# A decoder trunk on one core: the mixer's value products 512 columns wide over four open banks, and another order of its products

## The chip, the cores and the metric

One Trainium2 chip, of which the kernel uses one core. The metric is the device time of one execution in microseconds. The kernel before took 1346.19 us (median of 3 runs, 1345.29 to 1346.24). Engines are named as in the profile: PE is TensorE's matrix multiply, PEld its weight load, DVE is VectorE, ACT ScalarE, POOL GpSimd, SP SyncE, which here only starts transfers.

## The reference, cut to what matters

The trunk runs 512 tokens of width 1024 through two mixer layers, each followed by a dense SwiGLU layer, all in float32. The change touches only the first mixer, which has two groups of heads side by side:

```
h = rms_norm(x, w);  z, xbc, dt, q, k, v, g, gk = split(h @ w_in)
# group 1 (SSD): 16 heads of 64, here 8 pairs of 128 rows
xs, B, C = silu(conv(xbc));  dt, a from dt_raw
y = (causal C.B with decay) @ (xs*dt) + C @ states + d_skip*xs
y = rms_norm over 512 columns (y * silu(z))     # pairs 0-3, pairs 4-7
# group 2 (GLA): 4 heads, keys of 128, values of 256
o = (causal q.k with decay) @ v + q @ states
o = rms_norm over 256 columns (o) * silu(g)
x = x + concat(y, o) @ w_out
```

## The kernel before

Activations lie with features on the partitions and tokens along the free side, so a tile is 128 x 512. Every dense product is done in three passes over operands split in two (`mm3`, L167: high by high, high by low, low by high), and every 512 KB of weights goes through `weight` (L146): a transfer on SP's queue into `wraw` (two buffers), ACT's cast to `whi`, DVE's subtraction to `wlo` (three buffers each). A dense product of 128 output rows (`dense`, L172) is 24 products of 128 x 512 into one PSUM bank. There are eight banks: three that rotate for dense products (`acc`, L63) and, in the mixer, five for helpers (`aux`, L76: st, a1, xt once, a2 twice).

Group 1 runs in eight pairs f = 0..7. For each pair:

- `conv` (L409): the x product and the convolution on DVE, which gives `xs`; `z_gate` (L452): the z product and its SiLU, which gives `zg`.
- `core_in` (L458): decay factors `mt`, `ea`, `cd` on ACT, four transposes of `xs` on PE, and from these `xdt` and `xde` on DVE.
- `core_states` (L496): PE's state products (L501), then ACT's copy of the first state (L505) and four short DVE steps (L508), which give `hs`.
- `core_out` (L515): PE's outputs (L521, which waits until `hs` is complete, and L529), then four DVE steps to `y`.
- `finish` (L567): the squares of `y`, and after pairs 3 and 7 `group_norm` (L539): `rstd` (L197) sums over the partitions with two PE products (L205, L206), takes the inverse root in ten DVE steps (L210 to L220), then four scalings (L543), and each scaled tile is split by ACT (`mxh`, L140) and DVE (`mxl`, L141).

The scaled tiles feed the output projection: `out_round(r, ...)` (L309) is one quarter of it, 96 products in eight banks of 12, whose results DVE adds to the residual x (L319). Rounds 0 and 1 need pairs 0 to 3 and pairs 4 to 7, rounds 2 and 3 the GLA heads.

`values(h)` (L549) makes the 256 value columns of GLA head h with tokens on the partitions: for each of four token blocks one bank, 24 products that move 256 weight columns against a block of x, and ACT's scaled copy into `v` (L561). Four heads are 384 products.

The order on each engine is made at build time by a scheduler that takes, among what it holds for ready, what the program wrote first (weights are taken earlier than written, `AHEAD`). `order(i, behind)` adds that i stands behind another instruction on PE. Engines then run their own queue in order and wait at semaphores. In the program x and z products are written one pair ahead: in step f come `conv(f + 1)`, `core_states` of f, `z_gate(f + 1)`, `core_out` of f. `values(0)` is written in step 1, `values(1)` behind pair 3, round 0 in step 7, `values(2)` and `values(3)` behind pair 7. Group 2 follows: `project(0)` (L656: the q and k products of a head, 48 products), round 1, `project(1)`, then `inner` (L707) and `outer` head by head. Four products of the gate (L644, on bank st, from `gw`) are written at the start of group 2.

Of the kernel before, what the change touches and what calls it, by code (L numbers as in the profile page):

```python
# [8 lines left out]
F32 = mybir.dt.float32  # L9
# [9 lines left out]
P = 128  # L19
# [27 lines left out]
def kernel(ctx: ExitStack, tc: tile.TileContext, A, yT, stop=99):  # L47
# [28 lines left out]
    def aux(tag="st"):  # L76
        while isinstance(phase["tags"][tag], str):
            tag = phase["tags"][tag]
        return phase["p"].tile([P, T], F32, tag=tag, name=nm(tag), bufs=phase["tags"][tag])
# [66 lines left out]
    def weight(src, kc, m):  # L146

        with tc.high_priority(offset=AHEAD):
            return weight_now(src, kc, m)
# [17 lines left out]
    def mm3(out, ah, al, bh, bl, first, last):  # L167
        E.matmul(out, ah, bh, start=first, stop=False)  # L168
        E.matmul(out, ah, bl, start=False, stop=False)  # L169
        return E.matmul(out, al, bh, start=False, stop=last)  # L170
# [106 lines left out]
    def tok_scalar(R):  # L277

        ps = aux()
        for c in range(4):  # L280
            E.transpose(ps[:, c * P:(c + 1) * P], R[:, c * P:(c + 1) * P], ident)
        r = const.tile([P, 4], F32, tag="rtok", name=nm("rtok"))
        V.tensor_copy(r, ps.rearrange("p (c x) -> p c x", c=4)[:, :, 0])
        return r

    def gate(pool, tag, ps, R, bufs):

        h = pool.tile([P, T], F32, tag="cva", name=nm(tag + "h"), bufs=2)
# [20 lines left out]
    def out_round(r, parts, nxt=None):  # L309

        mms = []
        for m2 in range(4):
            w = weight(A["w_out"][r, m2], 4, 256)
            for j in range(2):
                m = 2 * m2 + j
                ps = acc()
                mms += dense(ps, (w[0][:, :, j * P:(j + 1) * P], w[1][:, :, j * P:(j + 1) * P]), parts)
                with tc.high_priority(offset=FREE):
                    V.tensor_tensor(X[m], X[m], ps, ALU.add)  # L319
                if nxt is not None:  # L320
                    nxt.add(m)
        return mms
# [8 lines left out]
    with tc.tile_pool(name="gkp", bufs=1) as gkp:  # L331
# [70 lines left out]
        with tc.tile_pool(name="ssd", bufs=2) as sp:  # L402
# [26 lines left out]
            def group(g):  # L429

                bank = (lambda: aux("a2")) if g == 0 else acc
                return conv(8 + g, "bT", 1, bank), conv(10 + g, "cT", 2, bank)
# [19 lines left out]
            def z_gate(f):  # L452
                w = weight(A["w_z"][f], KD, P)
                ps = acc()
                zmm[f] = dense(ps, w, xp)
                return gate(sp, "z", ps, R, 2)

            def core_in(f, xs, cb, behind=None):  # L458

# [36 lines left out]
            def core_states(part, btok, behind):  # L496

                f, xs, mt, ea, cd, xdt, xde = part
                pst = aux("a2")
                for c in range(3):  # L500
                    i = E.matmul(pst[:, c * P:(c + 1) * P], btok[:, c, :],  # L501
                                 xde[:, c].rearrange("p h e -> p (h e)"), start=True, stop=True)
                    order(i, behind, "states behind products that run until x is ready")
                hs = sp.tile([P, 3, P], F32, tag="hs", name=nm("hs"), bufs=1)
                S.copy(hs[:, 0, :], pst[:, 0:P])  # L505
                for c in (1, 2):
                    for h in range(2):
                        ready = V.scalar_tensor_tensor(hs[:, c, 64 * h:64 * h + 64],  # L508
                                               hs[:, c - 1, 64 * h:64 * h + 64],
                                               cd[:, c - 1, h:h + 1],  # L510
                                               pst[:, c * P + 64 * h:c * P + 64 * h + 64],
                                               ALU.mult, ALU.add)
                return hs, ready

            def core_out(part, state, zg, cT, behind):  # L515

                hs, ready = state
                f, xs, mt, ea, cd, xdt, xde = part
                po = aux("a2")
                for c in range(3):  # L520
                    i = E.matmul(po[:, c * P:(c + 1) * P], hs[:, c, :], cT[:, (c + 1) * P:(c + 2) * P],  # L521
                                 start=True, stop=True)
                    order(i, behind, "outputs behind products that run until the states are ready")
                    wait_for(i, ready, "outputs in one go")
                end = i
                pd = aux("a2")
                for c in range(4):
                    for h in range(2):
                        i = E.matmul(pd[64 * h:64 * h + 64, c * P:(c + 1) * P], xdt[:, c, h, :],  # L529
                                     mt[:, h, c, :], start=True, stop=True)  # L530
                        order(i, end, "outputs in one go")
                y = sp.tile([P, T], F32, tag="y", name=nm("y"), bufs=5)
                V.scalar_tensor_tensor(y, xs, col("d_skip", f), pd, ALU.mult, ALU.add)
                V.tensor_tensor(ea, po[:, :3 * P], ea, ALU.mult)
                V.tensor_tensor(y[:, P:], y[:, P:], ea, ALU.add)
                V.tensor_tensor(y, y, zg, ALU.mult)
                return y, i
# [10 lines left out]

            def values(h):  # L549

                mms = []
                wv = [weight(A["w_v"][h, j], 4, 256) for j in range(2)]
                v = gkp.tile([P, 4, 256], F32, name=f"v{h}")
                for i in range(4):
                    ps = acc()
                    for k in range(KD):
                        wh, wl = wv[k // 4]
                        xh, xl = xp[k]
                        mms.append(mm3(ps[:, :256], xh[:, i * P:(i + 1) * P], xl[:, i * P:(i + 1) * P],
                                       wh[:, k % 4, :], wl[:, k % 4, :], k == 0, k == KD - 1))  # L560
                    S.activation(v[:, i, :], ps[:, :256], AF.Copy, scale=rtok[:, i:i + 1])  # L561
                vt[h] = v
                return mms

            rounds, ys, sums_sq = [], [], []

            def finish(f, y):  # L567

                ys.append(y)
                sq = res.tile([P, T], F32, tag="sq", name=nm("ysq"), bufs=2)  # L570
                S.activation(sq, y, AF.Square)
                if f % 4:
                    V.tensor_tensor(sq, sums_sq[-1], sq, ALU.add)
                sums_sq.append(sq)
                if f % 4 == 3:
                    rounds.append(group_norm(f // 4, ys[-4:], sq))
# [15 lines left out]
            y, end = core_out(part, hs, zg[0], cT, zmm[2][7])  # L592
            part = core_in(1, xs[1], cb, end)
            finish(0, y)
            rtok = tok_scalar(R)
            v = values(0)
            hs = core_states(part, btok, v[5])
            y, end = core_out(part, hs, zg[1], cT, v[27])
            part = core_in(2, xs[2], cb, end)
            finish(1, y)  # L600
            for f in range(2, 8):
                cT_out = cT
                if f < 7:
                    if f == 3:
                        bc = group(1)
                    xs[f + 1] = conv(f + 1, "xs", 3)
                    hs = core_states(part, btok, mm[f + 1][4])
                    if f == 3:
                        cb, cT, btok = spread(*bc, mm[f + 1][-1])
                    zg[f + 1] = z_gate(f + 1)  # L610
                    last = zmm[f + 1][-1]
                else:
                    mms = out_round(0, rounds[0])
                    hs = core_states(part, btok, mms[3])
                    last = mms[11]
                y, end = core_out(part, hs, zg[f], cT_out, last)
                if f < 7:
                    part = core_in(f + 1, xs[f + 1], cb, end)
                finish(f, y)
                if f in (3, 7):  # L620
                    values(1 if f == 3 else 2)
            values(3)


        with tc.tile_pool(name="gla", bufs=2) as gp:
# [721 lines left out]
```

## Time and profile before

| | |
|---|---|
| median of 3 runs | 1346.19 us |
| the profiled execution | 1345.15 us, span 1343.0 us |
| PE busy | 1333.1 us (99%), 6506 products |
| PEld busy | 1094.3 us (81%) |
| DVE busy | 812.6 us (61%) |
| ACT busy | 564.5 us (42%) |
| moved by DMA | 122.23 MB, 91 GB/s |
| granted TensorE clock | 1.0 throughout |

The mixer's group 1 lies from the start of the span to about 223 us, group 2 from there to about 404 us. A row of the timeline has the start, the duration, the engine, the source line, the operation, the tile written and the tiles read (for PE the moving operand first, then the stationary one), sizes, and a count where several follow each other. The brackets hold the idle time of that engine ahead of it and what ended it. Durations of PE's products overlap, since the next one starts while the last one drains: what a product costs in a stream is the distance of the starts. One of the program's small float32 products appears as two passes in the profile (three L501 products as x6).

### The profile page before, as it was taken

Reading aid. Unit: us, or ns where it says so; the run is one execution under the profiler, and the core shown is the slowest. Engines: PE = TensorE matmul, PEld = TensorE weight load, DVE = VectorE, ACT = ScalarE, POOL = GpSimd, SP = SyncE. Lnnn points to the kernel's source line nnn. Section 1 sums busy time; section 2 is a strip of 40 time slices with the busy share of each in tenths; the row PEclk is TensorE's granted clock in tenths of the full one; section 3 lists DMA queues with packets and bytes.
Section 4 is the critical chain, followed back from the end, with each engine's and each line's share of the span. In section 5 each row is a group of like instructions: output and inputs, shape, how many; then the busy total and the mean of one; then the engine's idle time right before and its main releaser. Section 6 shows DMA issues by size and latency. Waiting matters only on the chain.

```text
span 1343.0 us, 16690 instructions
## 1 busy us (share of the span) xinstructions
PE 1333.1 (99%) x6506; PEld 1094.3 (81%) x6506; DVE 812.6 (61%) x1387; ACT 564.5 (42%) x958; POOL 7.8 (1%) x35
## 2 busy tenths in 40 slices
PE   9999999999999999999999999999999999999998
PEld 6888889888888888888888887777788888888887
DVE  7888977778976444444333469987674444443221
ACT  7675625544343232322222338886543322222111
POOL 0000000000000000000000000000000000000000
PEclk9999999999999999999999999999999999999999
DMA  5343232222223333333333321110223333333331
GB/s 180 127 126 95 81 100 86 96 66 63 80 96 98 104 94 94 94 94 98 95 101 103 91 79 47 53 48 32 63 92 97 94 94 95 104 100 94 114 108 61
DMA packets 36782, 122.23 MB, mean 91 GB/s; under 512 B 4768, under 2 KB 5792, under 8 KB 36704
## 3 DMA queue, kind: packets, MB, share of 16 engines
q1 hardware_dynamic: 35888, 120.72, 29.0%
q8 instruction: 51, 0.84, 0.3%
q10 hardware_dynamic: 816, 0.46, 0.1%
q14 instruction: 27, 0.22, 0.1%
HBM read 119.03 MB, written 2.13 MB: 90 GB/s over the span
## 4 chain that ended last, share of the span: by engine, by line
PE 87%; DVE 6%; ACT 5%; issue 1%; DMA 1%; POOL 0%; SPq 0%; DVEq 0%; POOLq 0%; ACTq 0%
PE acc L168 27%; PE acc L170 26%; PE acc L169 26%; PE sco L1095 1%; ACT whi L160 1%; ACT sc L1108 1%; DVE wlo L161 1%; PE po L1142 1%; PE ptr L1123 1%; DVE sc L1106 1%; PE a L529 1%; ACT mt L472 1%; PE a L753 1%; DVE cva L421 0%; PE a L521 0%
## 5 line engine op out<-in xcount | busy, mean ns | idle before, releaser
L160 ACT CAST whi<-wraw 128x1024 fp32r<-128x1024 f32 (+2 forms) x221 | 225.7, 1022 | 560.0 <-PE acc L169 430.4
L168 PE MATMUL acc<-xh,whi 128*128 128x512 f32 x1144 | 450.4, 394 | 0.2 <-ACT qT L1070 0.2
L169 PE MATMUL acc<-xl,whi 128*128 128x512 f32 x1144 | 446.6, 390 | 0.0
L170 PE MATMUL acc<-xh,wlo 128*128 128x512 f32 x1144 | 446.4, 390 | 0.0
L161 DVE TENSOR_TENSOR wlo<-wraw,whi 128x1024 fp32r<-128x1024 f32 (+2 forms) x221 | 262.0, 1187 | 150.4 <-ACT whi L160 150.0
L168 PEld LDWEIGHTS acc<-xh,whi 128*128 128x128 f32 x1144 | 215.0, 188 | 44.7 <-issue 0.8
L170 PEld LDWEIGHTS acc<-xh,wlo 128*128 128x128 f32 x1144 | 215.0, 188 | 44.8
L169 PEld LDWEIGHTS acc<-xl,whi 128*128 128x128 f32 x1144 | 215.1, 188 | 44.0 <-issue 0.4
L823 DVE TENSOR_TENSOR fu<-acc,R 128x512 f32<-128x512 f32 x44 | 30.4, 691 | 137.7 <-PE acc L170 137.7
L169 PE MATMUL acc<-fhl,whi 128*128 128x512 f32 x288 | 112.2, 390 | 0.0
L168 PE MATMUL acc<-fhh,whi 128*128 128x512 f32 x288 | 112.2, 390 | 0.0
L170 PE MATMUL acc<-fhh,wlo 128*128 128x512 f32 x288 | 112.2, 390 | 0.0
L820 DVE TENSOR_TENSOR fg<-acc,R 128x512 f32<-128x512 f32 x44 | 30.4, 691 | 89.3 <-PE acc L170 89.3
L169 PEld LDWEIGHTS acc<-fhl,whi 128*128 128x128 f32 x288 | 54.1, 188 | 11.3
L168 PEld LDWEIGHTS acc<-fhh,whi 128*128 128x128 f32 x288 | 54.1, 188 | 11.2
L170 PEld LDWEIGHTS acc<-fhh,wlo 128*128 128x128 f32 x288 | 54.1, 188 | 11.0
L168 PE MATMUL acc<-mxh,whi 128*128 128x512 f32 x128 | 49.9, 392 | 0.0
L169 PE MATMUL acc<-mxl,whi 128*128 128x512 f32 x128 | 49.8, 390 | 0.0
L170 PE MATMUL acc<-mxh,wlo 128*128 128x512 f32 x128 | 49.7, 390 | 0.0
L1108 ACT ACTIVATE sc<-sc,mx 128x128 f32<-128x128 f32 (+3 forms) x64 | 35.5, 558 | 11.7 <-DVE mx L1106 11.6
L1095 PE MATMUL sco<-kT,qT 96*128 96x256 f32 (+3 forms) x128 | 39.6, 440 | 0.7 <-ACT qT L1070 0.7
L837 DVE TENSOR_TENSOR x<-x,acc 128x512 f32<-128x512 f32 x16 | 11.0, 688 | 42.9 <-PE acc L170 42.9
(355 smaller groups left out, 1601.9 us busy)
## 6 DMA issues: line engine op xcount, KB each, us to landing
wraw<-in_w_gate_dram SPq DMA_DIRECT2D x44, 512.0 KB, 3.5
wraw<-in_w_up_dram SPq DMA_DIRECT2D x44, 512.0 KB, 3.5
wraw<-in_w_down_dram SPq DMA_DIRECT2D x32, 512.0 KB, 3.6
wraw<-in_w_out_dram SPq DMA_DIRECT2D x16, 512.0 KB, 3.5
wraw<-in_w_xbc_dram SPq DMA_DIRECT2D x12, 512.0 KB, 3.8
wraw<-in_w_down_dram SPq DMA_DIRECT2D x16, 384.0 KB, 3.1
wraw<-in_w_z_dram SPq DMA_DIRECT2D x8, 512.0 KB, 3.5
wraw<-in_w_v_dram SPq DMA_DIRECT2D x8, 512.0 KB, 3.5
```

The source lines that it names most:

```text
L160: S.copy(hi[:, :kc * m], r)
L161: i = V.tensor_tensor(lo[:, :kc * m], r, hi.bitcast(F32)[:, :kc * m], ALU.subtract)
L168: E.matmul(out, ah, bh, start=first, stop=False)
L169: E.matmul(out, ah, bl, start=False, stop=False)
L170: return E.matmul(out, al, bh, start=False, stop=last)
L472: S.activation(mt[:, h, c, :], acb[:, h, c * P:(c + 1) * P], AF.Relu, scale=-1.0, bias=act[:, c, 2 * f + h:2 * f + h + 1])
L529: i = E.matmul(pd[64 * h:64 * h + 64, c * P:(c + 1) * P], xdt[:, c, h, :], mt[:, h, c, :], start=True, stop=True)
L753: i = E.matmul(po[e][:, r * P:(r + 1) * P], v[:, r, e * P:(e + 1) * P], sc[:, r, :], start=True, stop=(r == 0))
L820: V.tensor_tensor(g, pg, R, ALU.mult)
L823: V.tensor_tensor(u, pu, R, ALU.mult)
L1095: i = E.matmul(ps[:, at:at + n], self.qts[j][:, b * P:(b + 1) * P], self.kts[j][:, :n], start=True, stop=True)
L1108: S.activation(sc[:, at:at + n], sc[:, at:at + n], AF.Exp, bias=mx[:, j:j + 1], scale=-1.0, accum_out=sm[:, j:j + 1])
```

## The change

Three things change, all in group 1.

1. `values(h)` now makes heads h and h + 1 together. Weights of both heads are laid side by side, so that a product moves 512 columns (256 of each head). A weight tile holds two of the eight k chunks for both heads; all four token blocks are open at once, in the three `acc` banks and a1, and the weight tiles are gone through one after the other. Each tile comes in two transfers of 256 KB in place of one of 512 KB. The four banks are complete only in the last quarter; then ACT copies each bank in two halves (eight copies in a row). There are 192 products of 512 columns in place of 384 of 256.
2. x and z products are written two pairs ahead: step f has `conv(f + 2)`, `core_states` of f behind its fifth product, `z_gate(f + 2)`, `core_out` of f. `zg` gets a third buffer.
3. Step 6 has no x and z products left and takes round 0; step 7 takes `values(2)` (heads 2 and 3). `values(0)` (heads 0 and 1) and the transposes for its token factors come behind pair 3. Nothing is written behind pair 7 any more: `project(0)` and round 1 follow at once.

```diff
-                return gate(sp, "z", ps, R, 2)
+                return gate(sp, "z", ps, R, 3)
...
-                wv = [weight(A["w_v"][h, j], 4, 256) for j in range(2)]
-                v = gkp.tile([P, 4, 256], F32, name=f"v{h}")
+                vt[h], vt[h + 1] = (gkp.tile([P, 4, 256], F32, name=f"v{h + e}") for e in range(2))
+                banks = [acc() for _ in range(3)] + [aux("a1")]
+                for q in range(4):
+                    raw = wp.tile([P, KD * P], F32, tag="wraw", name=nm("wraw"), bufs=2)
+                    with tc.high_priority(offset=AHEAD):
+                        for e in range(2):
+                            nc.sync.dma_start(raw.rearrange("p (k e m) -> p k e m", k=2, e=2)[:, :, e, :],
+                                              A["w_v"][h + e, q // 2, :, 2 * (q % 2):2 * (q % 2) + 2])
+                        wh, wl = parts(raw, 2, T)
+                    for i in range(4):
+                        for k in range(2):
+                            xh, xl = xp[2 * q + k]
+                            mms.append(mm3(banks[i], xh[:, i * P:(i + 1) * P], xl[:, i * P:(i + 1) * P],
+                                           wh[:, k, :], wl[:, k, :], (q, k) == (0, 0), (q, k) == (3, 1)))
                 for i in range(4):
-                    ps = acc()
-                    for k in range(KD):
...
-                    S.activation(v[:, i, :], ps[:, :256], AF.Copy, scale=rtok[:, i:i + 1])
-                vt[h] = v
+                    for e in range(2):
+                        S.activation(vt[h + e][:, i, :], banks[i][:, 256 * e:256 * e + 256], AF.Copy,
+                                     scale=rtok[:, i:i + 1])
...
-            rtok = tok_scalar(R)
-            v = values(0)
-            hs = core_states(part, btok, v[5])
-            y, end = core_out(part, hs, zg[1], cT, v[27])
-            part = core_in(2, xs[2], cb, end)
-            finish(1, y)
-            for f in range(2, 8):
+
+            for f in range(1, 8):
                 cT_out = cT
...
+                if f < 6:
+                    xs[f + 2] = conv(f + 2, "xs", 3)
+                    fill = mm[f + 2]
+                elif f == 6:
+                    fill = out_round(0, rounds[0])
                 else:
-                    mms = out_round(0, rounds[0])
-                    hs = core_states(part, btok, mms[3])
-                    last = mms[11]
+                    fill = values(2)
+                hs = core_states(part, btok, fill[4])
...
+                if f < 6:
+                    zg[f + 2] = z_gate(f + 2)
+                    last = zmm[f + 2][-1]
+                else:
+                    last = fill[11]
                 y, end = core_out(part, hs, zg[f], cT_out, last)
                 if f < 7:
                     part = core_in(f + 1, xs[f + 1], cb, end)
                 finish(f, y)
-                if f in (3, 7):
-                    values(1 if f == 3 else 2)
-            values(3)
+                if f == 3:
+                    rtok = tok_scalar(R)
+                    values(0)
```

Three places on PE show what the order became. The first is the value products. Before, behind pair 0's outputs, `whi` and `wlo` are the moved weights, `xh` and `xl` blocks of x, and `acc_133`, `acc_134` two token blocks, one bank after the other:

```order
L168 MATMUL acc_133_742<-whi_131_737,xh_19_155 128x256
L169 MATMUL acc_133_742<-wlo_132_738,xh_19_155 128x256
L170 MATMUL acc_133_742<-whi_131_737,xl_20_156 128x256
L168 MATMUL acc_134_768<-whi_128_731,xh_5_127 128x256
L169 MATMUL acc_134_768<-wlo_129_732,xh_5_127 128x256
L170 MATMUL acc_134_768<-whi_128_731,xl_6_128 128x256
L168 MATMUL acc_134_768<-whi_128_731,xh_7_131 128x256
L169 MATMUL acc_134_768<-wlo_129_732,xh_7_131 128x256
```

Now, behind pair 3's outputs, two token blocks (`acc_247`, `acc_248`) with the same weight tile:

```order
L168 MATMUL acc_247_1295<-whi_252_1302,xh_7_131 128x512
L169 MATMUL acc_247_1295<-wlo_253_1303,xh_7_131 128x512
L170 MATMUL acc_247_1295<-whi_252_1302,xl_8_132 128x512
L168 MATMUL acc_248_1296<-whi_252_1302,xh_5_127 128x512
L169 MATMUL acc_248_1296<-wlo_253_1303,xh_5_127 128x512
L170 MATMUL acc_248_1296<-whi_252_1302,xl_6_128 128x512
L168 MATMUL acc_248_1296<-whi_252_1302,xh_7_131 128x512
L169 MATMUL acc_248_1296<-wlo_253_1303,xh_7_131 128x512
```

The moved width went from 256 to 512, and a bank gets 6 products before the next bank's turn.

The second place is the last pair's outputs (L521 and L529). Before, they stand in the value products of head 2 (`acc_384`), with the rest of heads 2 and 3 behind them:

```order
L168 MATMUL acc_384_2091<-whi_382_2086,xh_17_151 128x256
L169 MATMUL acc_384_2091<-wlo_383_2087,xh_17_151 128x256
L170 MATMUL acc_384_2091<-whi_382_2086,xl_18_152 128x256
L521 MATMUL a2_361_2018<-cT_195_1134,hs_360_2012 128x128 x3
L529 MATMUL a2_362_2022<-mt_333_1845,xdt_336_1865 64x128 x8
L168 MATMUL acc_384_2091<-whi_382_2086,xh_19_155 128x256
L169 MATMUL acc_384_2091<-wlo_383_2087,xh_19_155 128x256
L170 MATMUL acc_384_2091<-whi_382_2086,xl_20_156 128x256
L168 MATMUL acc_385_2117<-whi_379_2080,xh_5_127 128x256
```

Now all 96 products of `values(2)` stand ahead of the pair's state products (L501), and the q product of GLA head 0 (`acc_398`) is around the outputs:

```order
L501 MATMUL a2_371_2050<-xde_353_1907,btok_212_1156 128x128 x3
L168 MATMUL acc_398_2172<-xh_5_127,whi_396_2168 128x512
L169 MATMUL acc_398_2172<-xl_6_128,whi_396_2168 128x512
L170 MATMUL acc_398_2172<-xh_5_127,wlo_397_2169 128x512
L168 MATMUL acc_398_2172<-xh_7_131,whi_396_2168 128x512
L169 MATMUL acc_398_2172<-xl_8_132,whi_396_2168 128x512
L170 MATMUL acc_398_2172<-xh_7_131,wlo_397_2169 128x512
L168 MATMUL acc_398_2172<-xh_9_135,whi_396_2168 128x512
L521 MATMUL a2_373_2060<-cT_198_1090,hs_372_2054 128x128 x3
L529 MATMUL a2_374_2064<-mt_349_1885,xdt_352_1905 64x128 x8
L169 MATMUL acc_398_2172<-xl_10_136,whi_396_2168 128x512
```

The 171 value products that stood behind the last outputs are gone from there, and the 96 wider ones of heads 2 and 3 stand ahead of them, 84 between pair 6's outputs and pair 7's states.

The third place is the start of round 1, where the scaled tiles of pairs 4 to 7 (`mxh`, `mxl`) are first read. Before, ahead of it is the end of the k product of GLA head 0 (`acc_413`):

```order
L168 MATMUL acc_413_2403<-xh_19_155,whi_411_2399 128x512
L169 MATMUL acc_413_2403<-xl_20_156,whi_411_2399 128x512
L170 MATMUL acc_413_2403<-xh_19_155,wlo_412_2400 128x512
L168 MATMUL acc_422_2447<-mxh_370_2059,whi_420_2443 128x512
L169 MATMUL acc_422_2447<-mxl_371_2060,whi_420_2443 128x512
L170 MATMUL acc_422_2447<-mxh_370_2059,wlo_421_2444 128x512
L168 MATMUL acc_422_2447<-mxh_372_2064,whi_420_2443 128x512
L169 MATMUL acc_422_2447<-mxl_373_2065,whi_420_2443 128x512
```

Now it is the same product (`acc_405`):

```order
L168 MATMUL acc_405_2211<-xh_19_155,whi_403_2207 128x512
L169 MATMUL acc_405_2211<-xl_20_156,whi_403_2207 128x512
L170 MATMUL acc_405_2211<-xh_19_155,wlo_404_2208 128x512
L168 MATMUL acc_414_2255<-mxh_382_2101,whi_412_2251 128x512
L169 MATMUL acc_414_2255<-mxl_383_2102,whi_412_2251 128x512
L170 MATMUL acc_414_2255<-mxh_382_2101,wlo_413_2252 128x512
L168 MATMUL acc_414_2255<-mxh_384_2106,whi_412_2251 128x512
L169 MATMUL acc_414_2255<-mxl_385_2107,whi_412_2251 128x512
```

What stands directly ahead has stayed. From the last pair's L529 to this place there were 171 value products, 48 products of `project(0)`, the gate's four products and L205 and L206; now there are 41 products of `project(0)` (17 + 24), L205 (two products into the k product) and L206 (20 products ahead of the round). The gate's products have moved into round 1, the first behind 18 of its products.

On DVE the steps from L210 to the last `mxl` stand in the same order as before, with two weight splits among them in both; on ACT the last bank's two copies of `values(2)` now stand directly ahead of pair 7's state copy (L505).

More of the change, by code (lines that the diff above doesn't have):

```diff
@@ L551, in values @@
                 mms = []
-                wv = [weight(A["w_v"][h, j], 4, 256) for j in range(2)]
-                v = gkp.tile([P, 4, 256], F32, name=f"v{h}")
-                for i in range(4):
-                    ps = acc()
-                    for k in range(KD):
[L557 to L561, printed above, removed]
-                vt[h] = v
+                vt[h], vt[h + 1] = (gkp.tile([P, 4, 256], F32, name=f"v{h + e}") for e in range(2))
[12 more added lines that the diff above has]
+                                           wh[:, k, :], wl[:, k, :], (q, k) == (0, 0), (q, k) == (3, 1)))
+                for i in range(4):
+                    for e in range(2):
+                        S.activation(vt[h + e][:, i, :], banks[i][:, 256 * e:256 * e + 256], AF.Copy,
+                                     scale=rtok[:, i:i + 1])
                 return mms
             rounds, ys, sums_sq = [], [], []
+            rtok = None
             def finish(f, y):
@@ L594 @@
             finish(0, y)
-            rtok = tok_scalar(R)
-            v = values(0)
-            hs = core_states(part, btok, v[5])
-            y, end = core_out(part, hs, zg[1], cT, v[27])
-            part = core_in(2, xs[2], cb, end)
-            finish(1, y)
-            for f in range(2, 8):
-                cT_out = cT
[L603 to L611, printed above, removed]
-                else:
-                    mms = out_round(0, rounds[0])
-                    hs = core_states(part, btok, mms[3])
-                    last = mms[11]
+            for f in range(1, 8):
+                cT_out = cT
+                if f == 3:
+                    bc = group(1)
+                if f < 6:
[3 more added lines that the diff above has]
+                    fill = out_round(0, rounds[0])
+                else:
+                    fill = values(2)
+                hs = core_states(part, btok, fill[4])
+                if f == 3:
+                    cb, cT, btok = spread(*bc, fill[-1])
+                if f < 6:
[3 more added lines that the diff above has]
+                    last = fill[11]
                 y, end = core_out(part, hs, zg[f], cT_out, last)
@@ L619 @@
                 finish(f, y)
-                if f in (3, 7):
-                    values(1 if f == 3 else 2)
-            values(3)
+                if f == 3:
+                    rtok = tok_scalar(R)
+                    values(0)
         with tc.tile_pool(name="gla", bufs=2) as gp:
```

## Prediction

> **What bounds the kernel now.** I read the page first, its head and its chain of work, and then the products by form.
>
> ```profile
> span 1343.0 us, 16690 instructions
> ## 1 busy us (share of the span) xinstructions
> PE 1333.1 (99%) x6506; PEld 1094.3 (81%) x6506; DVE 812.6 (61%) x1387; ACT 564.5 (42%) x958; POOL 7.8 (1%) x35
> ...
> PE 87%; DVE 6%; ACT 5%; issue 1%; DMA 1%; POOL 0%; SPq 0%; DVEq 0%; POOLq 0%; ACTq 0%
> ```
>
> PE bounds the kernel: 9.9 us of the span are idle, 87% of the chain is its own work. So the change can gain only by making PE's work shorter, and can lose wherever PE is made to wait. Busy time doesn't say how long that work is:
>
> ```profile
> L168 PE MATMUL acc<-whi,xh 128*128 128x256 f32 x128 | 36.6, 286 | 0.0
> ```
>
> By this row 384 value products would cost some 109 us. Durations overlap, though, so I take prices from the timeline, as distances of starts. The rows below are from it, for PE, DVE and ACT, from pair 7's states (L501) to the first scores of group 2 (L714).
>
> ```profile
> 197.05 0.83 PE L501 MATMUL a<-xde,btok 128*128 128x128 f32 x6
> 197.25 0.69 DVE L319 TENSOR_TENSOR x<-x,acc 128x512 f32<-128x512 f32 x1 [2.03 <-PE acc L170]
> 197.98 0.26 ACT L505 COPY hs<-a 128x128 f32<-128x128 f32 x1
> 199.25 0.85 DVE L508 SCALAR_TENSOR_TENSOR hs<-hs,cd,a 128x64 f32<-128x64 f32 x4
> 200.24 0.91 PE L521 MATMUL a<-cT,hs 128*128 128x128 f32 x6
> ...
> 202.10 0.39 PE L168 MATMUL acc<-whi,xh 128*128 128x256 f32 x1
> 202.76 0.47 ACT L561 ACTIVATE v<-acc,rtok 128x256 f32<-128x256 f32 x1 [4.52 <-PE acc L170]
> ...
> 206.67 0.50 PE L205 MATMUL st<-rsa,ones_r 128*128 128x512 f32 x1
> 207.48 0.41 PE L206 MATMUL st<-rsb,ones_r 128*128 128x512 f32 x1
> 207.73 0.28 PE L170 MATMUL acc<-whi,xl 128*128 128x256 f32 x1
> ...
> 213.44 1.23 DVE L161 TENSOR_TENSOR wlo<-wraw,whi 128x1024 fp32r<-128x1024 f32 x1
> ...
> 217.54 0.62 ACT L140 CAST mxh<-y 128x512 fp32r<-128x512 f32 x1 [0.89 <-DVE y L543]
> ...
> 221.99 0.69 DVE L141 TENSOR_TENSOR mxl<-y,mxh 128x512 fp32r<-128x512 f32 x1 [0.69 <-ACT mxh L140]
> 223.31 0.40 PE L168 MATMUL acc<-xh,whi 128*128 128x512 f32 x1
> 226.64 0.51 PE L644 MATMUL st<-gx,gw 80*128 80x512 f32 x1 [0.42 <-ACT gw L638]
> ...
> 233.65 0.40 PE L170 MATMUL acc<-xh,wlo 128*128 128x512 f32 x1
> ...
> 251.52 0.42 DVE L701 TENSOR_TENSOR kp<-kr,el 128x256 f32<-128x256 f32 x1
> ...
> 268.71 0.27 PE L714 MATMUL a<-qd,ki 128*64 128x64 f32 x1
> ```
>
> The reader should see two things. From 207.73 to 223.31 there are 130 products of 256 columns, 0.1198 us each; from 233.65 to 268.71 there are 154 of 512, 0.2277 us each. And after pair 7's outputs a long chain on DVE and ACT runs beside PE's products: from L206 at 207.48 to the first scaled tile split (`mxh`, done 218.16) 10.68 us, to the last `mxl` (done 222.68) 15.20 us. PE doesn't feel it, because value products and `project(0)` lie in between and round 1 starts only some 11 us after 223.31.
>
> **The change part by part.** I make the sum against the profiled execution, 1345.15 us; the median of the runs is 1.04 us above it, which I add at the end.
>
> *Wider value products.* Before: 384 x 0.1198 = 46.0 us. After: 192 x 0.2277 = 43.7 us. That is a gain of 2.3 us and nothing like the 34 us that busy times would promise.
>
> [...]
>
> The weights come in sixteen transfers of 256 KB. The trace has none of that shape; the nearest row is the present one.
>
> ```profile
> wraw<-in_w_v_dram SPq DMA_DIRECT2D x8, 512.0 KB, 3.5
> ```
>
> A weight tile lasts PE 24 x 0.2277 = 5.5 us and there are two raw buffers, so 3.5 us are hidden, and even 5 would be. I take 0, at most 1 us lost; a gain is excluded, since PE doesn't wait for weights now. Opening four banks costs nothing at the start: the third `acc` bank is needed only 12 products after the first, 2.7 us in which DVE empties it. At the end the first bank is complete 18 products (4.1 us) before the last, and ACT's copies of 0.47 us follow bank by bank. Behind pair 3 the copies also stand behind the group norm's fourth `mxh`, which comes at most 15.20 - 0.69 - 1.23 = 13.3 us behind that L206 (the chain above without its last subtraction and with one weight split less); PE has 59 products, 13.4 us, left there. I take 0, at most 1 us.
>
> *Two pairs ahead.* The same x and z work moves earlier; no step is added. In steps 1 to 5 PE gets 24 products (5.5 us) between a pair's states and its outputs, as in steps 2 to 6 before, and DVE has the convolution's steps between the four steps of `hs`, also as before. Pair 0 already waits:
>
> ```profile
> 66.48 0.91 PE L521 MATMUL a<-cT,hs 128*128 128x128 f32 x6 [0.62 <-ACT mt L474]
> ```
>
> With 13 wide products in front in place of 19 narrow ones (3.0 us for 2.3) it could wait less; but a z step of DVE now stands among the four of `hs`. I take 0, bounds 0.6 us either way. For pairs 1 to 6 I take 0.3 us lost in all; the bounds belong to a rival.
>
> *Round 0 in step 6.* The round stands as a whole ahead of pair 6's states, as it stood ahead of pair 7's, and 12 products (2.7 us) cover `hs` where 21 narrow ones (2.5 us) did. No change.
>
> *What covers the last pair's chain.* This is the term that decides. Let E be the end of the 96 products of `values(2)`. ACT empties the last bank first (0.2 us after E as at 197.25, then 2 x 0.47), copies the first state (0.26), DVE makes `hs` (0.85 and some 0.2 of hand-over): L521 can start at E + 2.5. PE is there after L501 and 7 products, at E + 0.83 + 1.59 = 2.4. Lost: 0.1.
>
> From L521 to L205 the trace has 206.67 - 200.24 = 6.43 us, paced by DVE and ACT. PE needs 202.10 - 200.24 = 1.86 for the passes and 19 x 0.2277 = 4.33 for products. Lost: 0.24. L206 follows in 0.8 us, as before.
>
> From L206 PE has 0.25 + 20 x 0.2277 = 4.80 us of work, and then stands before round 1, whose first product reads the first `mxh`: 10.68 us after L206. It waits 5.9 us. The products of a bank then go through the four tiles; the eleventh reads the last `mxl`, at 15.20. So the first 12 products end at 15.20 + 2 x 0.2277 = 15.66 where they would have ended at 4.80 + 2.73 = 7.53. Lost: 8.1 us. The chain holds two weight splits; without them (1.23 us each) 5.6 us would be lost. One of the two now waits for a cast which must wait for the k product's end, 4.8 + 0.2 + 1.05 = 6.05 us behind L206; before, it began 213.44 - 207.48 = 5.96 behind it, so this adds next to nothing.
>
> *What is late next.* The gate's products: before, PE lost 226.64 - 223.31 - 12 x 0.2277 = 0.6 us there; now they wait for `gw`, which DVE makes behind the first add of round 1, within 0.3 us of PE. Gain 0.3. The scores of group 2: from the fourth gate product, directly ahead of 233.65, to `kp` (done 251.94) the trace has 18.5 us, and to L714 35 us. After the change 100 products, 22.8 us, stand in between; 4 us of cover are left, so 0 lost.
>
> *Sum:* -2.3 + 0.3 + 0.1 + 0.24 + 8.1 - 0.3 = +6.1 us, 1351.3 by the profiled execution and 1352.3 by the median.
>
> **The rivals.**
>
> *PE comes back at half pace* (slower still). The trace's first products, after an idle start, are slow:
>
> ```profile
> 6.20 0.66 PE L169 MATMUL a<-xl,whi 128*48 128x512 f32 x1
> ...
> 9.87 0.63 PE L168 MATMUL a<-xh,whi 128*48 128x512 f32 x1
> 10.29 0.47 PE L169 MATMUL a<-xl,whi 128*48 128x512 f32 x1
> ```
>
> They start 0.42 us apart, and this lasts at least from 6.20 to 10.29. If the gap of 5.9 us brings this back, the last products of the first bank cost about 0.4 us more, and up to 4.1 us behind them run at half pace, another 2 at most. With some of that time spent in the waits I take +1.5: 1353.8. For it: the slow start. Against: no gap of that length is in the trace, and the wait of 0.62 us at 66.48 left no such trace. [...]
>
> *DVE falls behind in the open pairs.* Without the value products of step 1, pairs 1 to 3 come closer together, and where pairs follow each other DVE has little left:
>
> ```profile
> 140.00:160.00 20.00, 20.00 (x115) 16.64 (x115) 19.62 (x36) 12.98 (x27) 0.10 (x1) 1.00 0.23 70
> ```
>
> The columns are the window, then busy us and instructions of PE, PEld, DVE, ACT. If `hs` of pairs 1 to 6 came 0.5 us late each, 3 us would be added: 1355.3. Against: the same window has PE at 20.00, so DVE still keeps up.
>
> *The price is the busy time* (faster). If a 256-wide product really held PE for its 0.286 us, the new form would save some 34 us where the sum has 2.3, and the wait of 8 us would be paid from it: about 1320. It decides as soon as a narrow product costs more than 0.143 us. Against it stand the 130 starts 0.1198 us apart.
>
> *The wait is covered* (no change). If the chain to the split tiles were 6 us shorter than 15.20, because ACT has no value copies left in it, gain and loss would cancel: 1346. The rows show the chain paced by DVE's own steps, so I see at most the 2.5 us of the two splits.
>
> **How the numbers follow.** 0.2% (2.7 us) is about what a measurement of this kernel can tell from no change. Chances: the forecast 0.50, half pace 0.27, DVE behind 0.11, covered or half covered within 0.2% 0.06, busy price or anything else faster 0.06. Slower: 0.88. The range starts at 1349.0 (the chain without the splits, 5.6 us, and 0.8 us better elsewhere) and ends at 1357.0 (half pace at its full 2.4 us, and 2 us of late `hs`, copies and transfers).
>
> **What would show it.** Right: value products start 0.228 us apart; PE's idle time names round 1's products (L168 to L170 on `mxh`, `mxl`), released by ACT and DVE, some 8 us in all, between the k product and the second bank of round 1; no idle at L501 and L521 above 0.5 us. Half pace: starts 0.42 us apart right behind that gap. Wrong: no gap there, or gaps of the same size in pairs 1 to 6, or a spacing of the value products other than 0.228.

## The result and the profile after

The changed kernel takes 1351.92 us (median of 4 runs, 1351.43 to 1352.46), the kernel before in the same comparison 1345.97: a ratio of 1.0046, with a 95% interval of 1.0034 to 1.0058. It is slower by 6 us. The profiled execution took 1351.63 us. The head of its page:

```profile
span 1349.4 us, 16323 instructions
## 1 busy us (share of the span) xinstructions
PE 1332.2 (99%) x6314; PEld 1082.8 (80%) x6314; DVE 813.3 (60%) x1387; ACT 565.3 (42%) x958; POOL 7.8 (1%) x35
```

PE has 192 instructions fewer and is busy 0.9 us less, but the span is 6.4 us longer: its idle time grew from 9.9 to 17.2 us. The waits of PE, largest first (what PE waited for, in us in total, how often, the longest):

```profile
PE acc L168 <- ACT mxh L140: 5.7, 1, 5.7
...
PE a L521 <- DVE hs L508: 0.5, 1, 0.5
```

The first one is new: round 1's first product stands before its first tile. The same stretch in the timeline of PE, DVE and ACT, from the last pair's states to the first scores of group 2:

```profile
217.29 0.83 PE L501 MATMUL a<-xde,btok 128*128 128x128 f32 x6
219.58 0.85 PE L521 MATMUL a<-cT,hs 128*128 128x128 f32 x6
225.82 0.40 PE L205 MATMUL st<-rsa,ones_r 128*128 128x512 f32 x1
226.52 0.40 PE L206 MATMUL st<-rsb,ones_r 128*128 128x512 f32 x1
...
231.06 0.39 PE L170 MATMUL acc<-xh,wlo 128*128 128x512 f32 x1
...
236.49 1.95 ACT L140 CAST mxh<-y 128x512 fp32r<-128x512 f32 x3 [0.89 <-DVE y L543]
237.17 0.80 PE L168 MATMUL acc<-mxh,whi 128*128 128x512 f32 x1 [5.72 <-ACT mxh L140]
238.44 0.79 PE L169 MATMUL acc<-mxl,whi 128*128 128x512 f32 x1 [0.48 <-DVE mxl L141]
239.03 0.63 PE L170 MATMUL acc<-mxh,wlo 128*128 128x512 f32 x1
239.46 0.63 PE L168 MATMUL acc<-mxh,whi 128*128 128x512 f32 x1
...
240.94 0.69 DVE L141 TENSOR_TENSOR mxl<-y,mxh 128x512 fp32r<-128x512 f32 x1 [0.69 <-ACT mxh L140]
...
243.17 0.40 PE L168 MATMUL acc<-mxh,whi 128*128 128x512 f32 x1
...
274.72 0.27 PE L722 MATMUL a<-qd,ki 128*64 128x64 f32 x1
```

Behind the k product's last step the next one could start at 231.06 + 0.23, and PE stands until 237.17. The first tile's cast begins 9.97 us after L206, the last `mxl` is done 15.11 us after it. From 239.03 on the products start 0.43 us apart, and only from the second bank on at the old pace of 0.23 again. By the prices of the prediction, 12 products behind the k product would have put round 1's second bank at 226.52 + 0.23 + 32 x 0.2277 = 234.04; it starts at 243.17. So 9.1 us are lost here. Short windows at both ends of the slow products (us, PE busy us and instructions, granted clock, DMA share, GB/s) say why they are slow:

```profile
236.00:236.25 0.25, 0.00 (x0) 0.81 0.99 410
236.25:236.50 0.25, 0.00 (x0) 0.50 0.65 262
...
242.75:243.00 0.25, 0.25 (x2) 0.53 0.00 0
243.00:243.25 0.25, 0.25 (x3) 1.00 0.00 0
```

The granted clock is at half from 236.16 to 242.99 (a window's mean of 0.81 is half clock in the last 0.09 us of it, and 0.53 in the first 0.23). It falls 4.7 us after PE's last product has ended (231.06 + 0.39), while PE still stands, and PE comes back into it.

### The profile page after: what moved, and what is told of

Read it like the earlier page. It is cut to its first block, busy times and chain, and to the rows that moved or that the text cites. A ratio compares the mean times of both kernels' runs of the same rounds, so it can differ in the third digit from the quotient of the medians.

```text
span 1349.4 us, 16323 instructions
## 1 busy us (share of the span) xinstructions
PE 1332.2 (99%) x6314; PEld 1082.8 (80%) x6314; DVE 813.3 (60%) x1387; ACT 565.3 (42%) x958; POOL 7.8 (1%) x35
## 4 chain that ended last, share of the span: by engine, by line
PE 89%; DVE 5%; ACT 4%; issue 1%; DMA 1%; SPq 0%; DVEq 0%; ACTq 0%
PE acc L169 27%; PE acc L170 27%; PE acc L168 27%; PE sco L1103 2%; ACT sc L1116 1%; PE ptr L1131 1%; ACT whi L160 1%; PE po L1150 1%; DVE wlo L161 1%; PE a L529 1%; PE a L761 1%; DVE cva L421 0%; DVE st L1019 0%; PE a L521 0%; PE a L766 0%
```

## The experiments

Ten kernels were run, each compared with the kernel before on the same chip. The kernel before took 1345.97 us beside the changed kernel and 1345.44, 1345.62 and 1345.32 us beside the ten, so a difference between medians of two comparisons can be off by some 0.6 us. The expectations call the scores of GLA head 0 the scores of group 0. The first four take the change apart: the place of the second values, the width, the order, and other cover for the chain.

**The second values behind the last pair again.** All else is as in the changed kernel.

```
-                hs = core_states(part, btok, fill[4])
+                hs = core_states(part, btok, fill[4] if f < 7 else fill[-1])
...
+                if f == 7:
+                    values(2)
```

(Step 7 then makes no `fill` of its own.)

> The changed kernel, with the second values moved back behind the last pair: step 7 has no products of its own, and the 96 wide products of values(2) stand behind that pair's steps, so that 65 of them and the 48 of project(0), 113 products or 25.7 us, stand between the last pair's outputs and round 1. All else is as in the changed kernel: wide values, x and z two pairs ahead, round 0 in step 6. My theory (the loss is the cover that was taken from the last pair's norm chain): no wait for mxh or mxl at round 1, no stretch at half clock there, and the 9.1 us lost at round 1 come back: 1351.9 - 9.1 = 1342.8, between 1342.3 and 1344.0, below the kernel before. Rival A (the order of two pairs ahead costs time of its own, and the wait at round 1 only uncovered it): between 1346 and 1350. Rival B (the wait moves on to the next stage, the scores of group 2, which then come as late as now): 1350 to 1352.

Measured: 1343.62 us, a ratio of 0.9984 (0.9975 to 0.9993) to before; 8.3 us below the changed kernel by the medians, 7.8 when each is set against the kernel before in its own comparison. Its timeline on PE:

```profile
210.28 0.40 PE L206 MATMUL st<-rsb,ones_r 128*128 128x512 f32 x1
...
232.38 0.39 PE L168 MATMUL acc<-mxh,whi 128*128 128x512 f32 x1
...
265.74 0.27 PE L722 MATMUL a<-qd,ki 128*64 128x64 f32 x1
```

Round 1 comes 22.1 us after L206, where the chain needs 15.1; nothing waits, and the scores come 9.0 us earlier than in the changed kernel. So the loss is the place of the 96 value products, and nothing in the order of two pairs ahead. This version is also below the kernel before.

**The width alone**, in the order of before: two heads' wide values in step 1, the other two behind pair 7, the rest as it was.

```
+            v = values(0)
+            hs = core_states(part, btok, v[4])
...
+                    values(2)
```

> The kernel before with one part of the change, the values of two heads side by side over four open banks; the order of the pairs, round 0 and the place of the values in it stay as before. My theory (a narrow product costs its 0.1198 us, a wide one 0.2267): 2.5 us less than before, 1345.97 - 2.5 = 1343.5, between 1343.0 and 1344.3. Rival by the busy times (0.286 us a narrow product): 34 us less, 1312. [...] If the four banks held open cost something: 1346 or more.

Measured: 1345.01 us, ratio 0.9998 (0.9989 to 1.0007): no difference from before, where I expected 2.5 us. Two waits took most of the gain. With both heads' values in step 1 none are left behind pair 3, and DVE, which has the group norm there, is late for pair 5: it works on that norm until 155.7 and makes `xde` only at 157.29. PE's timeline there, and the first scores:

```profile
157.99 0.91 PE L501 MATMUL a<-xde,btok 128*128 128x128 f32 x6 [1.17 <-DVE xde L492]
...
267.17 0.27 PE L721 MATMUL a<-qd,ki 128*64 128x64 f32 x1
```

At the scores 1.5 of the 2.5 us are left (268.71 before); behind them PE comes to the GLA states (L744) before DVE has masked the scores (`sc`, L729), and at the end of the span 0.6 us are left (1342.4 against 1343.0). From the waits of the same kernel:

```profile
PE xt L744 <- DVE sc L729: 0.6, 1, 0.6
```

So this run doesn't price the width; the last run below does.

**The order alone**, with one head's 256 columns after the other's.

```
-            def values(h):
+            def values_of(h):
...
+            def values(h):
+                return values_of(h) + values_of(h + 1)
```

> The other part of the change alone: its order (x and z two pairs ahead, round 0 in step 6, values(2) in step 7 ahead of the last pair's states), with the values as one head's 256 columns after the other's, as before. My theory: the order has the whole loss and the wide form the gain of 2.5 us, so 1351.9 + 2.5 = 1354.4, between 1353.5 and 1355.3, with the same wait at round 1 and the same stretch of half clock behind it. Rival (the four banks held open, emptied late, are what makes the last pair's chain late): 1346 to 1350, with a wait at round 1 some microseconds shorter.

Measured: 1356.41 us, 1.0080 (1.0066 to 1.0094); 4.5 us above the changed kernel, more than the width's price and above the range that I expected. The rival is out: the four banks don't make the last pair late. On the contrary, the kernel with the narrow form has it later. Its timeline of PE, ACT and DVE:

```profile
219.40 0.83 PE L501 MATMUL a<-xde,btok 128*128 128x128 f32 x6
219.97 1.04 ACT L160 CAST whi<-wraw 128x1024 fp32r<-128x1024 f32 x1
220.90 0.27 ACT L505 COPY hs<-a 128x128 f32<-128x128 f32 x1
221.04 1.23 DVE L161 TENSOR_TENSOR wlo<-wraw,whi 128x1024 fp32r<-128x1024 f32 x1 [0.53 <-ACT whi L160]
...
228.52 1.22 DVE L161 TENSOR_TENSOR wlo<-wraw,whi 128x1024 fp32r<-128x1024 f32 x1 [1.27 <-ACT whi L160]
...
...
232.08 0.39 PE L206 MATMUL st<-rsb,ones_r 128*128 128x512 f32 x1
241.74 0.79 PE L168 MATMUL acc<-mxh,whi 128*128 128x512 f32 x1 [7.88 <-ACT mxh L140]
```

A weight cast of 1.04 us stands ahead of the first state's copy (in the changed kernel it stood behind it), and its split of 1.23 us ahead of `hs`; a second cast (at 227.44) and its split stand among the squares of `y`. L206 comes 12.7 us after L501 where it came after 9.2. PE has the same work for a longer chain, and waits 7.9 us, 2.2 more than in the changed kernel; with the 2.3 of the form this is the 4.5. Why the casts fall at these places was not followed.

**Other cover: project(1) ahead of round 1.**

```
             q0, _ = project(0)
-            out_round(1, rounds[1])
             q1, last = project(1)
+            out_round(1, rounds[1])
```

> The changed kernel with project(1) written ahead of round 1 in place of behind it: 48 products (10.9 us) more stand between the k product of project(0) and round 1; the order ahead of them, up to L206 and the 20 products behind it, stays. My theory: the products cover what is left of the chain (5.7 us to the first mxh, and the last mxl 9.9 us behind the end of the k product), so no wait at round 1 and no half clock: 1351.9 - 9.1 = 1342.8, between 1342.3 and 1345 since the gate's products then come earlier against their DVE steps and the projections of group 1 must be kept longer. Rival A (the DVE steps of project(1) get in the way of the norm and the wait stays): 1347 to 1352. Rival B (the stall moves to the scores of group 0 or to the sums of round 1): 1345 to 1350.

Measured: 1352.69 us, 1.0054 (1.0041 to 1.0067). My number was wrong by 10 us, and the time lies above both rivals' ranges; a stall that moves on, as in rival B, is what happened, in a place that I had not named. DVE's and PE's timeline:

```profile
242.11 0.68 DVE L644 TENSOR_TENSOR gw<-w,wt 16x512 fp32r<-16x512 f32 x1
...
243.41 0.80 PE L652 MATMUL st<-gx,gw 80*128 80x512 f32 x1 [6.48 <-ACT gw L646]
```

Between two of the 48 products stands the gate's first one. It needs `gw`. A DVE step and two ACT casts make it, and both stand behind the norm's last `mxl`: the DVE step in DVE's queue, the casts (L646, which the wait names) behind a POOL memset that was released by that `mxl`. So PE waits for the same chain through another tile, and the product that waits blocks the cover behind it: the next one of project(1) starts at 244.00.

The second four runs price the clock and the chain, and go after that cover.

**Idle products in the gap**, 24 and 12 of them, which nobody reads.

```
+            ps = aux("xt")
+            for j in range(24):
+                i = E.matmul(ps, ones_r, xp[0][0], start=True, stop=True)
+                order(i, end, "idle products in the gap")
```

> The changed kernel with 24 products more on PE in the gap between the k product and round 1. They multiply tiles that are there already into a bank that nobody reads, so they compute nothing and only keep PE at work: 24 x 0.2277 = 5.5 us of the gap of 5.7. My theory (of the 9.1 us lost at round 1 about 1.1 come from the half clock that the gap brings on, 8.0 from the chain): the wait before the first product of round 1 shrinks to about 0.3 us, the products behind it start 0.228 apart in place of 0.427 wherever they do not wait for a tile, the granted clock stays at 1.00, and round 1's second bank starts 1.1 us earlier: 1351.9 - 1.1 = 1350.8. Rival (the slow starts are the pace of the mxl tiles, not of the clock): spacing and time as now, 1351.9. If the whole delay were the clock's: 1348 or less.

> The changed kernel with 12 such products in the gap (2.7 us; nobody reads what they write), so that PE still stands idle for about 3.0 us before round 1. If the clock falls only behind a gap of more than about 5 us: as with 24, 1350.8, starts 0.228 apart, granted clock 1.00. If a gap of 3 us is enough: the stretch of half clock stays, perhaps shorter, 1351.3 to 1351.9. The chain's 8.0 us stay lost either way.

Measured: 1350.52 us with 24, 1.0039 (1.0025 to 1.0053), and 1352.00 with 12, 1.0049 (1.0035 to 1.0064). With 24, PE's timeline:

```profile
226.48 0.40 PE L206 MATMUL st<-rsb,ones_r 128*128 128x512 f32 x1
...
239.02 0.39 PE L168 MATMUL acc<-mxh,whi 128*128 128x512 f32 x1
239.25 0.39 PE L169 MATMUL acc<-mxl,whi 128*128 128x512 f32 x1
...
241.68 0.50 PE L169 MATMUL acc<-mxl,whi 128*128 128x512 f32 x1 [0.22 <-DVE mxl L141]
242.01 0.40 PE L170 MATMUL acc<-mxh,wlo 128*128 128x512 f32 x1
242.41 0.50 PE L168 MATMUL acc<-mxh,whi 128*128 128x512 f32 x1
```

The starts are 0.23 apart, the granted clock stays at 1.00, and the second bank starts 15.93 us after L206 in place of 16.65: the half clock costs 0.7 us, not the 1.1 I put on it; of the other 0.4, 0.3 are starts of 0.33 and 0.40 us behind a wait in place of 0.23. Most of the slow stretch is hidden, since at full clock the same products wait for their tiles (0.77, 0.39 and 0.22 us in this run). The chain's 8.4 us stay lost.

With 12 products, PE's timeline:

```profile
236.99 0.50 PE L168 MATMUL acc<-mxh,whi 128*128 128x512 f32 x1 [2.92 <-ACT mxh L140]
238.27 0.58 PE L169 MATMUL acc<-mxl,whi 128*128 128x512 f32 x1 [0.77 <-DVE mxl L141]
...
239.50 0.63 PE L169 MATMUL acc<-mxl,whi 128*128 128x512 f32 x1
239.93 0.63 PE L170 MATMUL acc<-mxh,wlo 128*128 128x512 f32 x1
```

A gap of 2.9 us, one product and a wait of 0.8 were enough for the half clock: the starts are 0.43 apart again, here for 3.4 us. The second bank starts at 242.48, 16.1 us after L206. Over the five runs of this kernel the mean granted clock lies between 0.996 and 0.999 and the time between 1350.58 and 1352.54; the one with 24 has 1.000 in all five.

**The splits held back**: two weight splits leave the chain, since a weight's split now stands behind `norm_end`, the norm's last subtraction on DVE.

```
+            if r == 1 and m2:
+                hold.append(norm_end[0])
             w = weight(A["w_out"][r, m2], 4, 256)
+            hold.clear()
```

> The changed kernel in which the splits of round 1's second to fourth weights must stand behind the last subtraction of the group norm on DVE. Two splits of 1.22 us leave the chain from L206 to round 1's tiles; PE's order there stays but for the gate's products. By the chain's terms the first mxh and the last mxl come 2.4 us earlier and the gap shrinks from 5.7 to 3.3 us. If a gap of 3.3 us is too short for the half clock: 1351.9 - 2.4 - 1.1 = 1348.4. If not: 1349.5. Rival (the splits lie beside a wait of the chain for ACT or PE, so taking them out changes nothing): 1351.9. A new wait, 0.5 us or more, for the second weight's split at round 1's third bank would speak for having moved it too late.

Measured: 1352.24 us, 1.0047 (1.0034 to 1.0060): no gain in the time. The chain did become shorter. PE and DVE:

```profile
227.87 0.39 PE L206 MATMUL st<-rsb,ones_r 128*128 128x512 f32 x1
236.49 0.79 PE L168 MATMUL acc<-mxh,whi 128*128 128x512 f32 x1 [3.66 <-ACT mxh L140]
...
240.27 0.69 DVE L141 TENSOR_TENSOR mxl<-y,mxh 128x512 fp32r<-128x512 f32 x1 [0.68 <-ACT mxh L140]
...
243.61 0.50 PE L168 MATMUL acc<-mxh,whi 128*128 128x512 f32 x1 [0.78 <-DVE x L322]
...
245.21 0.67 DVE L687 SCALAR_TENSOR_TENSOR qd<-acc,R 128x512 f32<-128x512 f32 x1
```

The last `mxl` is done 13.1 us after L206 in place of 15.1: the splits were on the chain, for 2.0 of their 2.4 us. But the second bank starts 15.7 us after L206, only 0.9 earlier: the clock is at half behind a gap of 3.7 us too, and those products now have to reuse the PSUM bank of round 1's first 12 and wait 0.8 us until DVE has added it to x. DVE, which took `qd` out of its bank at 241.67 in the changed kernel, does so at 245.21 here, behind the two splits. This execution also entered the stretch late: pair 0's outputs start at 68.11 in place of 66.78. The time settles nothing; the rows bear out the chain's term.

**The gate's products later**, on top of project(1) ahead of round 1.

```
+            mms = out_round(1, rounds[1])
+            order(gates[0], mms[3], "gate products behind the first bank of round 1")
```

> The run with project(1) ahead of round 1, and one edit more: the first of the gate's four products stands behind the first bank of round 1 in place of at the earliest place that the scheduler finds. In the run without it PE stood 6.5 us at that product, which waited for gw, a tile that DVE makes behind the norm's last subtraction. My theory (the cover of 48 products was enough for the tiles of round 1, and the gate's product was the only thing in the way): no wait of more than 0.5 us between L206 and round 1, no half clock, first scores some 9 us earlier than in the changed kernel: 1342.8, up to 1345.5 if the scores of group 0, which now come 22 us behind the gate's products, wait for them. Rival (one wait is again replaced by the next): 1347 to 1352, with the next waiting place named by the waits.

Measured: 1352.96 us, 1.0055 (1.0042 to 1.0068). Wrong again, and the rival right in kind (its range ends at 1352). DVE and PE:

```profile
243.36 0.67 DVE L684 SCALAR_TENSOR_TENSOR qd<-acc,R 128x512 f32<-128x512 f32 x1
...
244.17 0.76 PE L168 MATMUL acc<-xh,whi 128*128 128x512 f32 x1 [6.60 <-DVE qd L684]
```

The product that waits is now the first one of project(1)'s k. There are three `acc` banks; the q and the k of project(0) and the q of project(1) fill them, and the first comes free only when DVE takes `qd` out, which also stands behind the norm's chain in its queue. So the 24 products of the q were cover, and the 24 of the k were not.

The last two runs test that account and price the width alone.

**A fourth bank** for that k product, on top of the run before.

```
-                ps = acc()
+                ps = aux("a1") if h == 1 else acc()
                 last = dense(ps, w, xp)[-1]
```

> The run with project(1) ahead of round 1 and the gate's products behind round 1's first bank, and one edit more: the k product of project(1) goes into the bank a1, which is free there, in place of one of the three acc banks. In the run without it PE stood 6.6 us at that k product, since its bank held the q of project(0), which DVE takes out behind the norm's chain. My theory (cover that needs a bank back from DVE is no cover while DVE is in the chain): the 48 products now run through, and round 1's first bank needs the bank of that q, which comes about 1.3 us behind the end of project(1). One wait of 1 to 2 us naming acc at round 1 and DVE's qd, no half clock: 1342.8 + 1.5 = 1344.3, between 1343.3 and 1346. Rival (the wait for tiles or scores just moves on again): 1349 to 1353.

Measured: 1345.68 us, 1.0001 (0.9992 to 1.0010): 7.3 us less than the run without it, by the name of a bank. The only wait of PE over 0.5 us in the stretch is the one expected:

```profile
244.09 0.47 PE L168 MATMUL acc<-mxh,whi 128*128 128x512 f32 x1 [1.17 <-DVE qd L684]
```

The time lies in the range expected, and the granted clock is 1.00 throughout. So 48 products are enough, where they don't need DVE. The first scores start at 267.16, 199.8 us after pair 0's outputs at 67.36; with the values behind the last pair it was 199.0. Why the whole is 2.1 us longer than there was not followed further.

**The width, with nothing waiting at round 1**: against the changed kernel, the second values behind the last pair again, and all of them narrow.

```
-            def values(h):
+            def values_of(h):
...
+                if f == 7:
+                    values(2)
```

> The run with the second values behind the last pair (1343.6), with the values again as one head's 256 columns after the other's: 384 narrow products in place of 192 wide ones, in the same places, and nothing waits at round 1. The pure price of the form. My theory (0.1198 a narrow and 0.2267 a wide product): 384 x 0.1198 - 192 x 0.2267 = 2.5 us more, 1346.1, between 1345.4 and 1346.9, as the kernel before, so that the order of two pairs ahead by itself costs nothing. Rival (by the run with the wide form alone the form is worth 0.4 us, and the order the rest): 1344.0. [...]

Measured: 1344.05 us, 0.9992 (0.9983 to 1.0001). With the wide form it was 1343.62, 0.9984: 0.4 us apart by the medians and 1.1 by the ratios, whose intervals overlap, where I expected 2.5. Where the price went shows by position. PE's timeline, first of the wide form (its first scores, at 265.74, are shown above), then of the narrow one:

```profile
66.76 0.91 PE L521 MATMUL a<-cT,hs 128*128 128x128 f32 x6 [0.33 <-DVE hs L508]
...
320.36 1.10 PE L745 MATMUL xt<-v,kt 128*128 128x256 f32 x4 [0.69 <-DVE sc L730]
```

```profile
66.36 0.91 PE L521 MATMUL a<-cT,hs 128*128 128x128 f32 x6 [0.41 <-DVE hs L508]
...
267.66 0.27 PE L717 MATMUL a<-qd,ki 128*64 128x64 f32 x1
```

From pair 0's outputs to the first scores it is 198.98 us wide and 201.30 narrow: the wide form gains 2.3 us there, the forecast's figure. As its execution was 0.4 us late at pair 0, it is 1.9 us ahead at the scores. Then PE, being earlier, waits 0.7 us for DVE's masked scores at 320.36, a wait that the narrow form doesn't have; behind it 1.05 us are left (the narrow form has that product at 321.41), and at the end of the spans 0.7 (1341.1 and 1341.8). The end-to-end difference alone looks like the rival that gave the form 0.4 us; the stretch that holds the products has 2.3.

## Why the prediction was right, point by point

The forecast was 1352.3 us, the median is 1351.92. The mechanism is the one forecast, shown by undoing it: with the second values behind the last pair the time falls by 8.3 us. That the number came within 0.4 us is in part luck: the terms came out with errors of both signs.

- *Wider value products*, -2.3: the spacing is 0.2267 us (72 products from 200.97 to 217.29) against 0.1198, and the stretch to the scores is 2.3 us shorter by it. Right; the run of the width alone showed it can be lost again to waits that it uncovers. The rival by busy times is out.
- *Two pairs ahead*, +0.3: from pair 0's outputs to the first scores the run with narrow values behind the last pair takes 201.30 us, the kernel before 268.71 - 66.48 = 202.23. So the order by itself gained 0.9 us up to there, an error of 1.2. The small terms at the last pair, +0.1 and +0.24, came out at about nothing: L521 comes 2.29 us after L501 and L205 6.24 after L521, without a wait. At L501 and L521 of pairs 1 to 6 PE shows no wait; DVE did not fall behind.
- *Cover of the last pair's chain*, +8.1: the places are right, the first `mxh` done 10.6 us after L206 and the last `mxl` 15.11 where I had 10.68 and 15.20. Lost were 9.1 us. The step that was too small is "the first 12 products end at 15.20 + 2 x 0.2277": the second bank starts 16.65 us after L206 in place of 15.66. Of this 1.0 us, 0.7 are the half clock's and 0.3 slower starts behind waits, which the run with 24 idle products has too.
- *PE comes back at half pace*: this rival's mechanism happened, in full (0.43 us apart, granted clock 0.50). Its price was wrong: 0.7 us by the 24 idle products, not 1.5, because most of the slow stretch lies under the wait for the `mxl` tiles. "Against: no gap of that length is in the trace" was true, and no argument. By the prediction's own signs this rival came true beside the forecast; only its price kept the time near the forecast.
- *From the profiled execution to the median*, +1.04: here the median lies 0.3 us above the profiled execution. By its own time the sum gave 1351.3, and the execution took 1351.63.
- *What is late next*, -0.3 at the gate and 0 at the scores: no wait at the gate's products above 0.3 us (0.6 were lost there before), nor at the scores of group 2. Right.

Together, from pair 0's outputs to the first scores: -2.3 - 0.9 + 9.1 = +5.9 us, and the two profiles have 207.94 - 202.23 = +5.7.

What stays open: why the difference between the changed kernel and the one with 24 idle products is 1.4 us in the medians (1.0 when each is set against its own kernel before) and 0.7 by position. Their runs overlap (1351.43 to 1352.46, 1349.89 to 1352.17), so it may be spread.

## What to carry to other kernels

Work that covers a chain is worth something only behind the chain's start: a filler that is moved from behind a chain to ahead of it is lost as cover, even if every engine has the same work. It costs what the products left behind don't cover: 113 behind the last outputs hid the chain here, 41 left 9.1 us of it open. And a filler covers a chain only if it needs nothing that stands behind the chain in some engine's queue, neither a tile (6.5 us of waiting for `gw`) nor the bank it writes to (6.6 us for the bank that `qd` reads): the value products, which ACT empties, did; the projections, which DVE empties, did only as far as the banks lasted. A gain on the engine that bounds the kernel has to be followed to the next meeting with another engine: 2.3 us were there at the scores, and 0.4 to 0.7 at the end.

## What the hardware showed

In six kernels the half clock lasted 3.42, 6.83 or 10.24 us, read from windows of 0.25 us as above (PE's stop is the end of its last product ahead of the gap; in the last row, of the last idle product):

| kernel | PE stops | clock falls | clock back | at half |
|---|---|---|---|---|
| the changed kernel | 231.45 | 236.16 | 242.99 | 6.83 |
| the splits held back | 232.84 | 236.23 | 243.06 | 6.83 |
| the gate's products later | 237.57 | 242.57 | 249.40 | 6.83 |
| project(1) ahead of round 1 | 236.93 | 238.94 | 249.18 | 10.24 |
| the order alone, narrow values | 233.86 | 237.68 | 247.92 | 10.24 |
| 12 idle products | 234.07 | 238.54 | 241.96 | 3.42 |

The longer two are 2 and 3 times the shortest, and the fall comes 2.0 to 5.0 us after the stop, so that a different share of the half clock falls into the gap itself (1.0 us of it in the changed kernel, where PE starts again at 237.17, and 4.5 with project(1) ahead of round 1, where it starts at 243.41). In the last row one product and the start of another, at 236.99 and 238.27, lie between the stop and the fall. What sets the moment of the fall and the lengths, no run shows.
